# First stage of a transformer layer: conditioning rows in three small buffers, and their transfers moved from SyncE's queue to GpSimd's

## The chip, the cores and the metric

The kernel runs on one core of a Trainium2 chip. The metric is the device time of one execution in microseconds (us). Five engines work side by side, each through its own instructions in order: TensorE (PE in the profile, its weight loads PEld), VectorE (DVE), ScalarE (ACT), GpSimd (POOL) and SyncE (SP), which only issues transfers. Transfers (DMAs) from HBM to the core's memory SBUF run on 16 DMA engines that all queues share.

## The reference, cut to what matters

One layer over 256 tokens of width 2048, in float32. A condition vector `c` makes nine modulation vectors of 2048 numbers each (three triples of shift, scale and gate); a feed-forward block, a token mixer and a second feed-forward block follow, each with a layer norm behind it.

```python
def _swiglu(h, w_in, w_out):
    gate, up = jnp.split(h @ w_in, 2, axis=-1)
    return (jax.nn.silu(gate) * up) @ w_out

def _layer(x, c, w_ada, b_ada, ffn1_w_in, ffn1_w_out, ln1_g, ln1_b, w_in, ...):
    ada = (jax.nn.silu(c) @ w_ada + b_ada)[:, None, :]
    sh1, sc1, g1, sh2, sc2, g2, sh3, sc3, g3 = jnp.split(ada, N_ADA, axis=-1)
    h = _swiglu(_modulate(x, sh1, sc1), ffn1_w_in, ffn1_w_out)
    x = _layernorm(ALPHA * x + 0.5 * (1 + g1) * h, ln1_g, ln1_b)
    h = _token_mixer(_modulate(x, sh2, sc2), w_in, ...)
    x = _layernorm(ALPHA * x + (1 + g2) * h, ln2_g, ln2_b)
    h = _swiglu(_modulate(x, sh3, sc3), ffn2_w_in, ffn2_w_out)
    x = _layernorm(ALPHA * x + 0.5 * (1 + g3) * h, ln3_g, ln3_b)
    return x
```

`w_ada` is 2048 x 18432, `ffn1_w_in` and `ffn2_w_in` 2048 x 11264, the output weights 5632 x 2048. Nearly all bytes are weights, each read once.

## The kernel before, in words

**Weights.** Every weight comes in 1 MB transfers into one of three places of the tag "raw" (line 362). ScalarE rounds it to a high part `hi`, VectorE subtracts to get the low part `lo` (`split`, lines 141 to 143), each in six places, and TensorE makes three products of every pair (`mm3`, lines 372 to 375), so that float32 accuracy is kept. A "raw" place is free again when both of its `lo` parts are made.

**Ada rows.** A modulation vector pair or a half gate takes 16 rows (each 128 x 1024, 512 KB) of `w_ada`. VectorE multiplies each by one column of silu(c) and adds it up (`ada_acc`, lines 153 to 158); TensorE then sums over the partitions. In all there are 288 rows: 64 in the first stage, 224 behind it. Outside the first stage, `ada_pair` (lines 173 to 192) and `ada_gate` (lines 194 to 212) load rows into two places of the tag "araw". They are generators: `pump` (line 228) lets them make so many rows for every megabyte of weights that the other stages use, `need` (line 238) makes them finish a part. `pinned` orders what they issue on VectorE behind the latest weight split. A gate part also loads its bias over GpSimd's queue (line 203).

**First stage** (lines 656 to 786). The first feed-forward block starts before its modulation is whole. The 2048 inputs are cut into four quarters `j`. Quarter `j` needs 512 columns of shift and scale; `first_ada(j)` makes them from 16 rows and then modulates. The loop runs 12 calls of `first_in(j, i)` for each `j`; each uses 1 MB of weights (`first_w`, line 722) in 48 matmuls of 256 columns. Beside quarter `j` runs `first_ada(j + 1)`, one step after most calls (not after `i` = 4, 9, 11). A step loads two rows and adds up both. In steps 2 and 5 of 8 the two rows go to "araw", in the other six together into one "raw" place, the same three that the weights use (lines 663 to 675). Beside `j` = 3 the smaller mixer inputs are loaded and `pump` begins.

**Order.** All transfers but the six bias loads are issued by SyncE, in order: a transfer that waits for its place holds up all that come behind it. The order of the instructions on each engine is set when the program is built.

Of the kernel before, what the change touches and what calls it, by code (L numbers as in the profile page):

```python
# [7 lines left out]
F32 = mybir.dt.float32  # L8
# [7 lines left out]
P = 128  # L16
# [18 lines left out]
def layer_kernel(  # L35
# [8 lines left out]
    V, S, G_, PE, SP = nc.vector, nc.scalar, nc.gpsimd, nc.tensor, nc.sync  # L44
# [16 lines left out]
    ap = ctx.enter_context(tc.tile_pool(name="ap", bufs=1))  # L61
# [88 lines left out]
    def pair_cols(v, j):  # L150
        return w_ada[0, :, v * D:(v + 2) * D].rearrange("k (v n) -> k v n", v=2)[:, :, j * 512:(j + 1) * 512]

    def ada_acc(acc, raw, k):
        if k == 0:
            V.tensor_scalar_mul(acc, raw, csil[:, k:k + 1])
        else:
            V.scalar_tensor_tensor(out=acc, in0=raw, scalar=csil[:, k:k + 1], in1=acc,  # L157
                                   op0=ALU.mult, op1=ALU.add)


    def ada_split(acc, tag):
        ahi = ap.tile([P, 512], F32R, tag="ahi", name=f"ahi{tag}")
        alo = ap.tile([P, 512], F32R, tag="alo", name=f"alo{tag}")
        split(acc, ahi, alo)
        return ahi, alo

    def ada_sum(parts, tag):
        bc = aux_tile(f"bc{tag}")
        for i in range(2):
            PE.matmul(bc, onesr, parts[i], start=i == 0, stop=i == 1)  # L170
        return bc

    def ada_pair(v, js):
        for j in js:
            src = pair_cols(v, j)
            acc = ap.tile([P, 2, 512], F32, tag="acc", name=f"acc{v}_{j}")
            for k in range(KD):
                raw = ap.tile([P, 2, 512], F32, tag="araw", bufs=2, name=f"ar{v}_{j}_{k}")
                SP.dma_start(raw, src[k * P:(k + 1) * P])
                ada_acc(acc, raw, k)  # L180
                yield
            for i in range(2):
                parts = ada_split(acc[:, i, :], f"{v}_{j}_{i}")
                for _ in range(2):
                    yield PAUSE
                bc = ada_sum(parts, f"{v}_{j}_{i}")
                dg = ap.tile([P, 4, P], F32, tag="alo", name=f"dg{v}_{j}_{i}")
                V.tensor_tensor(out=dg, in0=bc.rearrange("p (a b) -> p a b", b=P),
                                in1=ident.unsqueeze(1).to_broadcast([P, 4, P]), op=ALU.mult)
                V.tensor_reduce(out=scsh[:, v + i, j * 4:(j + 1) * 4], in_=dg, axis=AX.X, op=ALU.add)  # L190
            cs = scsh[:, v:v + 2, j * 4:(j + 1) * 4]
            V.tensor_tensor(out=cs, in0=cs, in1=bcol[:, v:v + 2, j * 4:(j + 1) * 4], op=ALU.add)

    def ada_gate(v, s):
        for j in range(2):
            c0 = v * D + j * 1024
            acc = ap.tile([P, 1024], F32, tag="acc", name=f"acc{v}_{j}")
            for k in range(KD):
                raw = ap.tile([P, 1024], F32, tag="araw", bufs=2, name=f"ar{v}_{j}_{k}")
                SP.dma_start(raw, w_ada[0, k * P:(k + 1) * P, c0:c0 + 1024])  # L200
                ada_acc(acc, raw, k)
                yield
            G_.dma_start(gate[:, j * 1024:(j + 1) * 1024], b_ada[0:1, c0:c0 + 1024].to_broadcast([P, 1024]))
            for i in range(2):
                parts = ada_split(acc[:, i * 512:(i + 1) * 512], f"{v}_{j}_{i}")
                for _ in range(2):
                    yield PAUSE
                bc = ada_sum(parts, f"{v}_{j}_{i}")
                gs = gate[:, j * 1024 + i * 512:j * 1024 + (i + 1) * 512]
                V.scalar_tensor_tensor(out=gs, in0=bc, scalar=1.0, in1=gs, op0=ALU.add, op1=ALU.add)  # L210
                if s != 1.0:
                    V.tensor_scalar_mul(gs, gs, s)
# [176 lines left out]
    def ffn_in(w, xT, hT, j0, tag, npump):  # L389
        for j in range(j0, DFF // 256):  # L390
            ps = [mm_tile(f"gu_{tag}{j}_{f}") for f in range(2)]
            for gu in range(2):
                last = gu and j == DFF // 256 - 1
                cols_form_a(w, gu * DFF + j * 256, [p[:, gu * T:(gu + 1) * T] for p in ps], xT,
                            f"{tag}i{j}_{gu}", (lambda: None) if last else npump)
            for f in range(2):
                sg = sm.tile([P, T], F32, tag="sg", bufs=2, name=f"sg_{tag}{j}_{f}")
                S.activation(sg, ps[f][:, :T], AF.Silu)
                pin["h"] = V.tensor_tensor(out=hT[:, 2 * j + f, :], in0=sg, in1=ps[f][:, T:], op=ALU.mult).ins
        for _ in range(2):  # L400
            npump()
# [242 lines left out]
    def at(rate):  # L644
        return lambda: pump(rate)

    hp = tc.alloc_tile_pool(name="hp1", bufs=1)
    hT = hp.tile([P, KF, T], F32, name="hT1")
    h0 = [hp.tile([P, 2, T], F32R, name=f"h0_{i}") for i in range(2)]
    xp = tc.alloc_tile_pool(name="xp1", bufs=1, **right)  # L650
    npool = tc.alloc_tile_pool(name="np1", bufs=1, **right)
    xT = new_xT("f1")
    W1 = ffn1_w_in[0]


    def first_ada(j, ws=iter(())):
        src = pair_cols(0, j)
        if j % 2:
            acc = ap.tile([P, 2, 512], F32, tag="acc", name=f"acc0_{j}")
        else:  # L660
            acc = gate[:, :1024].rearrange("p (v n) -> p v n", v=2)
        for kk in range(8):
            if kk % 3 == 2:
                raws = []
                for h in range(2):
                    k = 2 * kk + h
                    raw = ap.tile([P, 2, 512], F32, tag="araw", bufs=2, name=f"ar0_{j}_{k}")
                    SP.dma_start(raw, src[k * P:(k + 1) * P])
                    raws.append(raw)
            else:  # L670
                raw = wp.tile([P, 2, 2, 512], F32, tag="raw", bufs=3, name=f"ar0_{j}_{kk}")
                for h in range(2):
                    k = 2 * kk + h
                    SP.dma_start(raw[:, h], src[k * P:(k + 1) * P])
                raws = [raw[:, h] for h in range(2)]
            for h in range(2):
                k = 2 * kk + h
                if k < KD - 1:
                    ada_acc(acc, raws[h], k)
                else:  # L680
                    for b in range(2):
                        bs = slice(b * 256, (b + 1) * 256)
                        ada_acc(acc[:, :, bs], raws[h][:, :, bs], k)
            if kk == 5:
                mb = modulate_both(0, j, rs0, xT)
            if kk in (5, 6):
                next(mb)
            yield
        cps = aux_tile(f"cp{j}"), mm_tile(f"cq{j}")

        def column(q):
            cp = cps[q % 2][:, q:q + 2]
            for v in range(2):
                PE.matmul(cp[:, v:v + 1], acc[:, v, q * P:(q + 1) * P], ones[:, 0:1], start=True, stop=True)
            k = 4 * j + q
            V.tensor_tensor(out=scsh[:, 0:2, k:k + 1], in0=cp.unsqueeze(2), in1=bcol[:, 0:2, k:k + 1], op=ALU.add)

        column(0)
        next(mb)
        column(1)  # L700
        next(mb)
        next(mb)
        column(2)
        next(ws, None)
        next(mb)
        column(3)
        next(mb)
        next(ws, None)
        for _ in mb:
            pass  # L710
        yield
# [10 lines left out]
    def first_w(j, i):  # L722
        c0 = (i % 2) * DFF + i // 2 * 512
        for k, hi, lo in load_w(W1[j * 512:(j + 1) * 512, c0:c0 + 512], 4, 512, f"s{j}_{i}"):
            yield 4 * j + k, hi, lo
# [52 lines left out]
    for j in range(4):  # L778
        fa = first_ada(j + 1) if j < 3 else load_mixer_smalls()
        for i in range(NS):  # L780
            first_in(j, i, ws if i + j == 0 else first_w(j, i))
            for _ in range(i not in (4, 9, 11)):
                with pinned():
                    next(fa, 0)
            if j == 3 and i > 2:
                pump(R_F)
    npool.release()
    ffn_in(W1, xT, hT, NS, "f1", at(R_IN))
    xp.release()
    lnp = tc.alloc_tile_pool(name="ln1", bufs=1, **right)  # L790
# [45 lines left out]
    fence, _, xs = boundary(*ent["f"], lgb, 3, "1", xT, entry_of(mo_load, mow, 3, 6), KD)  # L836
# [326 lines left out]
    for j in (2, 3, 0, 1):  # L1163
        ps = form_a_pair(C_FQ + j * 256, C_FK + j * 256, f"f{j}")
        for i in range(2):
            h = 2 * j + i
# [88 lines left out]
    for j in range(2, 10):  # L1255
# [8 lines left out]
        for f in range(2):  # L1264
            i = 2 * j + f
# [11 lines left out]
    for j in range(2, 10):  # L1277
# [7 lines left out]
        for f in range(2):  # L1285
            i = 2 * j + f
# [51 lines left out]
```

## Time and profile before

| | us |
|---|---|
| median of three runs | 1966.2 (1963.88 to 1972.04) |
| the profiled execution, its own time | 1965.57 |
| span of the profiled execution | 1963.8 |
| PE busy / DVE busy / ACT busy / POOL busy | 1896.5 / 1495.8 / 961.1 / 6.3 |
| first matmul of the first stage, last one | 37.8, 320.5 |

HBM was read at 259 GB/s over the span (506.71 MB). A profile is read here by engine and by stage: a share of busy time over the span says little where stages have different limits. In rows of windows, the count behind "x" is the number of instructions that touched the window; for PE it is the better measure, since the ends of matmuls are modelled.

### The profile page before, as it was taken

The page shows a single profiled execution, that of the slowest core. Times are in us where ns is not written, and L with a number is a line of the kernel's source. Part 1 is how long each engine was busy: PE and PEld are TensorE (multiplying, and loading weights), DVE is VectorE, ACT ScalarE, POOL GpSimd, SP SyncE. Part 2 cuts the span into 40 slices and gives each one's busy share as a digit, 9 for nine tenths or more (in the row PEclk, how much of TensorE's full clock was granted, in tenths as well). Part 3 has the DMA queues.
Part 4 walks back from the last instruction along what each step waited for, and adds up shares of the span by engine and source line. Part 5 has one row for each costly group of instructions (what it writes and reads, how often), then busy time and mean ns, then how long its engine had stood idle before and what let it go on. Part 6 is the DMA issues. An engine that isn't in the chain of part 4 may idle for free.

```text
span 1963.8 us, 32259 instructions
## 1 busy us (share of the span) xinstructions
PE 1896.5 (97%) x13057; PEld 1727.6 (88%) x13057; DVE 1495.8 (76%) x1878; ACT 961.1 (49%) x1396; POOL 6.3 (0%) x17
## 2 busy tenths in 40 slices
PE   3999999999999999899999998999999999999997
PEld 3999999999988888588999786899999999988885
DVE  7788889777788897678888688777766655555776
ACT  3644354443454554745755544555444444444553
POOL 0000000000000000000000000000000000000000
PEclk9999999999999999999999999999999999999999
DMA  9998978899898786489888784888777765655552
GB/s 331 342 315 278 314 253 289 290 305 326 281 343 303 268 303 208 140 292 319 270 300 278 273 285 151 285 292 274 241 248 249 261 216 190 236 193 193 193 193 86
DMA packets 301820, 510.89 MB, mean 260 GB/s; under 512 B 10818, under 2 KB 158690, under 8 KB 300648
## 3 DMA queue, kind: packets, MB, share of 16 engines
q1 hardware_dynamic: 300808, 505.70, 76.2%
q0 software_dynamic: 864, 3.15, 0.5%
q8 instruction: 102, 1.67, 0.4%
q14 instruction: 46, 0.38, 0.0%
HBM read 506.71 MB, written 2.10 MB: 259 GB/s over the span
## 4 chain that ended last, share of the span: by engine, by line
PE 83%; DVE 8%; DMA 5%; ACT 2%; issue 2%; SPq 0%; DVEq 0%; ACTq 0%
PE gu_f L374 8%; PE gu_f L375 8%; PE gu_f L373 8%; PE o_f L373 8%; PE o_f L375 8%; PE o_f L374 8%; PE s L373 3%; PE s L375 3%; PE s L374 3%; DMA raw_s<-in_ffn_w_in_dram 2%; DVE lo_s L143 2%; PE fs L375 1%; PE fs L374 1%; PE fs L373 1%; PE o_mx L373 1%
## 5 line engine op out<-in xcount | busy, mean ns | idle before, releaser
L157 DVE SCALAR_TENSOR_TENSOR acc<-ar,csil,acc 128x1024 f32<-128x1024 f32 x242 | 307.8, 1272 | 74.6 <-DMA ar<-in_w_ada_dram 72.9
L373 PE MATMUL s<-xhi_f,hi_s 128*128 128x256 f32 x768 | 215.0, 280 | 3.0 <-ACT hi_s L142 3.0
L375 PE MATMUL s<-xhi_f,lo_s 128*128 128x256 f32 x768 | 214.4, 280 | 1.9 <-DVE lo_s L143 1.9
L374 PE MATMUL s<-xlo_f,hi_s 128*128 128x256 f32 x768 | 214.2, 279 | 0.0
L375 PE MATMUL gu_f<-xhi_f,lo_f2i 128*128 128x256 f32 x768 | 212.0, 276 | 0.0
L373 PE MATMUL gu_f<-xhi_f,hi_f2i 128*128 128x256 f32 x768 | 212.0, 276 | 0.0
L374 PE MATMUL gu_f<-xlo_f,hi_f2i 128*128 128x256 f32 x768 | 212.0, 276 | 0.0
L143 DVE TENSOR_TENSOR lo_f2i<-raw_f2i,hi_f2i 128x1024 fp32r<-128x1024 f32 x96 | 117.6, 1225 | 91.4 <-ACT hi_f2i L142 91.4
L373 PE MATMUL gu_f<-xhi_f,hi_f1i 128*128 128x256 f32 x640 | 176.8, 276 | 0.0
L375 PE MATMUL gu_f<-xhi_f,lo_f1i 128*128 128x256 f32 x640 | 176.7, 276 | 0.0
L374 PE MATMUL gu_f<-xlo_f,hi_f1i 128*128 128x256 f32 x640 | 176.7, 276 | 0.0
L142 ACT CAST hi_f2i<-raw_f2i 128x1024 fp32r<-128x1024 f32 x96 | 100.8, 1050 | 135.4 <-PE gu_f L374 124.6
L373 PEld LDWEIGHTS s<-xhi_f,hi_s 128*128 128x128 f32 x768 | 146.2, 190 | 3.5 <-ACT hi_s L142 3.4
L142 ACT CAST hi_s<-raw_s 128x1024 fp32r<-128x1024 f32 x96 | 96.6, 1049 | 107.0 <-DMA raw_s<-in_ffn_w_in_dram 85.9
L375 PEld LDWEIGHTS s<-xhi_f,lo_s 128*128 128x128 f32 x768 | 145.9, 190 | 2.9 <-DVE lo_s L143 2.8
L374 PEld LDWEIGHTS s<-xlo_f,hi_s 128*128 128x128 f32 x768 | 146.4, 191 | 0.0
L374 PEld LDWEIGHTS gu_f<-xlo_f,hi_f2i 128*128 128x128 f32 x768 | 144.2, 188 | 0.2
L373 PEld LDWEIGHTS gu_f<-xhi_f,hi_f2i 128*128 128x128 f32 x768 | 144.2, 188 | 0.2
L375 PEld LDWEIGHTS gu_f<-xhi_f,lo_f2i 128*128 128x128 f32 x768 | 144.2, 188 | 0.0
L142 ACT CAST hh<-hT 128x512 fp32r<-128x512 f32 x130 | 80.0, 622 | 127.9 <-PE o_f L374 126.6
L143 DVE TENSOR_TENSOR lo_f2o<-raw_f2o,hi_f2o 128x1024 fp32r<-128x1024 f32 x88 | 107.7, 1224 | 44.9 <-ACT hi_f2o L142 44.8
L143 DVE TENSOR_TENSOR lo_s<-raw_s,hi_s 128x1024 fp32r<-128x1024 f32 x96 | 114.5, 1221 | 30.6 <-ACT hi_s L142 30.6
(452 smaller groups left out, 5385.2 us busy)
## 6 DMA issues: line engine op xcount, KB each, us to landing
ar<-in_w_ada_dram SPq DMA_DIRECT2D x288, 512.0 KB, 5.4
raw_s<-in_ffn_w_in_dram SPq DMA_DIRECT2D x48, 1024.0 KB, 6.1
raw_f2i<-in_ffn_w_in_dram SPq DMA_DIRECT2D x48, 1024.0 KB, 5.2
raw_f1o<-in_ffn_w_out_dram SPq DMA_DIRECT2D x44, 1024.0 KB, 7.4
raw_f2o<-in_ffn_w_out_dram SPq DMA_DIRECT2D x44, 1024.0 KB, 5.1
raw_f1i<-in_ffn_w_in_dram SPq DMA_DIRECT2D x40, 1024.0 KB, 7.7
raw_mxo<-in_w_out_dram SPq DMA_DIRECT2D x16, 1024.0 KB, 6.1
raw_fh<-in_ffn_w_in_dram SPq DMA_DIRECT2D x16, 1024.0 KB, 7.3
```

The source lines that it names most:

```text
L142: S.copy(hi, src)
L143: return V.tensor_tensor(out=lo, in0=src, in1=hi.bitcast(F32), op=ALU.subtract)
L157: V.scalar_tensor_tensor(out=acc, in0=raw, scalar=csil[:, k:k + 1], in1=acc, op0=ALU.mult, op1=ALU.add)
L373: PE.matmul(o, ah, bh, start=start, stop=False)
L374: PE.matmul(o, ah, bl, start=False, stop=False)
L375: PE.matmul(o, al, bh, start=False, stop=stop)
```

## The change

Three edits.

1. `first_ada` for `j` >= 1 no longer uses "raw". Its rows go to three places of 512 KB: two of "araw", and one of a new pool `ep1` (tag "aw") for every third row. The pool is released behind the first stage. `first_ada(0)` is as it was.
2. A step for `j` >= 1 is now one row, not two; the loop takes one or two steps after each call by a list of 12 numbers, 17 steps in all (16 rows and the tail) where it took 9 (8 pairs and the tail).
3. The transfers of ada rows are issued from GpSimd's queue: in `first_ada` for `j` >= 1, and in `ada_pair` and `ada_gate`, so 272 of the 288 rows.

```diff
@@ ada_pair
-                SP.dma_start(raw, src[k * P:(k + 1) * P])
+                G_.dma_start(raw, src[k * P:(k + 1) * P])
@@ ada_gate
-                SP.dma_start(raw, w_ada[0, k * P:(k + 1) * P, c0:c0 + 1024])
+                G_.dma_start(raw, w_ada[0, k * P:(k + 1) * P, c0:c0 + 1024])
@@ before the first stage
+    ep = tc.alloc_tile_pool(name="ep1", bufs=1)
@@ first_ada
         for kk in range(8):
-            if kk % 3 == 2:
+            if j or kk % 3 == 2:
                 raws = []
                 for h in range(2):
                     k = 2 * kk + h
-                    raw = ap.tile([P, 2, 512], F32, tag="araw", bufs=2, name=f"ar0_{j}_{k}")
-                    SP.dma_start(raw, src[k * P:(k + 1) * P])
+                    where, tag, n = (ep, "aw", 1) if j and k % 3 == 2 else (ap, "araw", 2)
+                    raw = where.tile([P, 2, 512], F32, tag=tag, bufs=n, name=f"ar0_{j}_{k}")
+                    (G_ if j else SP).dma_start(raw, src[k * P:(k + 1) * P])
                     raws.append(raw)
+                    if j and h == 0:
+                        ada_acc(acc, raw, k)
+                        yield
...
-            for h in range(2):
+            for h in range(j > 0, 2):
@@ the loop over j and i
-            for _ in range(i not in (4, 9, 11)):
+            for _ in range((2, 1, 2, 1, 2, 2, 1, 2, 1, 2, 1, 0)[i] if j < 3 else i not in (4, 9, 11)):
                 with pinned():
                     next(fa, 0)
...
     npool.release()
+    ep.release()
```

## The prediction

> **What bounds the kernel now.** I read the page's totals first, then windows of ten us through the first stage, then the waits there. On the page, TensorE is busy almost throughout.
>
> ```profile
> span 1963.8 us, 32259 instructions
> PE 1896.5 (97%) x13057; PEld 1727.6 (88%) x13057; DVE 1495.8 (76%) x1878; ACT 961.1 (49%) x1396; POOL 6.3 (0%) x17
> ```
>
> So 1963.8 - 1896.5 = 67 us of TensorE idleness is all that a change of transfers could win, most of it before the first matmul and in the norms. What the first stage holds of it shows in windows (columns: window and length, then busy time and count of PE, PEld, DVE, ACT, POOL, granted clock, DMA share, GB/s).
>
> ```profile
> 50.00:60.00 10.00, 10.00 (x90) 10.00 (x89) 8.00 (x7) 5.01 (x7) 0.00 (x0) 1.00 0.93 342
> 150.00:160.00 10.00, 9.45 (x84) 9.25 (x82) 8.38 (x10) 0.04 (x1) 0.00 (x0) 1.00 0.94 322
> 160.00:170.00 10.00, 7.93 (x52) 7.72 (x53) 8.66 (x9) 6.99 (x8) 0.00 (x0) 0.83 0.85 276
> 210.00:220.00 10.00, 9.67 (x85) 9.47 (x85) 9.96 (x11) 4.00 (x4) 0.00 (x0) 1.00 0.93 317
> 230.00:240.00 10.00, 8.72 (x74) 8.32 (x74) 7.76 (x10) 4.41 (x5) 0.00 (x0) 1.00 1.02 361
> 240.00:250.00 10.00, 8.96 (x79) 8.76 (x78) 8.88 (x11) 5.58 (x6) 0.00 (x0) 1.00 0.90 306
> 38.00:258.00 220.00, 214.50 (x1831) 212.91 (x1832) 183.87 (x205) 104.40 (x135) 0.67 (x1) 0.99 0.88 305
> ```
>
> The full rate is 90 matmuls in 10 us. The five poor windows lack 6, 38, 5, 16 and 11 of them, 76 in all, at 9.0 per us 8.4 us: the ceiling of what this stage can win. The clock fell to 0.83 in the worst one, so part of its price is the clock. Who was late:
>
> ```profile
> ACT hi_s L142 <- DMA raw_s<-in_ffn_w_in_dram: 85.9, 28, 10.2
> SPq L363 <- DVE lo_s L143: 67.0, 29, 5.1
> SPq L363 <- DVE acc L157: 16.7, 6, 4.5
> SPq L363 <- DVE gate L157: 12.2, 3, 6.1
> ```
>
> These are waits between 40 and 258 us (total, times, longest). ScalarE waits for weights, and SyncE's weight transfers (L363) wait 16.7 + 12.2 = 28.9 us for an ada row to be added up (L157), because the row sits in a weight's place or at the queue's head. SyncE's queue around the worst stall:
>
> ```profile
> 147.61 0.37 SPq L668 DMA_DIRECT2D ar<-in_w_ada_dram  x1
> 148.74 1.21 SPq L674 DMA_DIRECT2D ar<-in_w_ada_dram  x2
> ...
> 153.47 10.59 SPq L363 DMA_DIRECT2D raw_s<-in_ffn_w_in_dram  x4
> 167.15 0.88 SPq L674 DMA_DIRECT2D ar<-in_w_ada_dram  x2
> ...
> 160.22 1.99 ACT L142 CAST hi_s<-raw_s 128x1024 fp32r<-128x1024 f32 x2 [10.18 <-DMA raw_s<-in_ffn_w_in_dram]
> ```
>
> Two rows take a "raw" place at 148.74; the next weight goes out only at 153.47, and ScalarE, idle for 10.18 us, starts at 160.22. The rows cause the stall.
>
> **The change part by part.** *Places.* A quarter is 12 x 48 = 576 matmuls, 64 us at 9.0 per us. Before, 12 weights and 6 row pairs share three places: 64 / 18 x 3 = 10.7 us for each use. After, 12 weights: 16 us. The landings, in the order weights (whole stage), ada rows (40 to 258 us), ada rows (330 to 745 us), GpSimd's two bias loads (170 to 335 us), all six bias loads, min/median/max; last the row additions of 330 to 745 us (count | busy, mean ns | idle before):
>
> ```profile
> DMA to landing us min/median/max: 4.9/6.1/9.2
> ...
> DMA to landing us min/median/max: 3.9/5.8/9.0
> ...
> DMA to landing us min/median/max: 3.9/5.3/9.3
> ...
> DMA to landing us min/median/max: 4.3/6.7/9.0
> ...
> L203 POOL DMA_DIRECT2D gate<-in_b_ada_dram x6: 527/530/667, 178.6 to 1208.5; - x6
> ...
> DMA to landing us min/median/max: 4.1/5.0/9.0
> ...
> L157 DVE SCALAR_TENSOR_TENSOR acc<-ar,csil,acc 128x1024 f32<-128x1024 f32 x78 | 100.0, 1281 | 36.1 <-DMA ar<-in_w_ada_dram 35.9
> ```
>
> Two rows' landing of 5.8 and their two additions of 1.28 fill 8.4 of 10.7 us before any wait in VectorE's order, and half of 16, so the stalls by place go. But at 230 to 250 us the DMA share was 1.02 and 0.90: there the engines themselves were full, and those 16 + 11 matmuls, with the 5 at 210 (share 0.93), I leave. What I take away is 6 + 38 = 44 matmuls, 4.9 us; bounds 0 and 8.4.
>
> *Rows in three small places.* 16 rows through three places in 64 us leave 12 us for each use; the worst bias landing, 9.0, and one addition of 1.28 are 10.3. VectorE does the same additions. Cost 0, hidden in that 12 us; if landings pass 10.7 us VectorE waits at the row, and behind it the `lo` parts, then TensorE.
>
> *Issue.* 272 issues at GpSimd's 0.53 us are 144 us on an engine busy for 6.3 us: nothing waits for it, cost 0. What stands in that queue besides: the six bias loads and the mask's two instructions.
>
> ```profile
> 330.14 0.53 POOL L203 DMA_DIRECT2D gate<-in_b_ada_dram  x1 [150.92 <-DVE hT L748]
> 673.16 0.53 POOL L203 DMA_DIRECT2D gate<-in_b_ada_dram  x1 [342.49 <-DVE o_f L436]
> 834.53 0.81 POOL L855 MEMSET mask<- 128x256 f32 x1 [45.41 <-DVE xlo_mx L355]
> ...
> 1023.78 9.42 SPq L200 DMA_DIRECT2D ar<-in_w_ada_dram  x4
> ```
>
> The bias loads waited there for `gate` to be free. Behind their part's 16 rows they come later than that: the one of 673.16 moves behind the last row of its part, which SyncE issued about 1025, one of the four rows of that line. So no row queues behind a waiting bias, and the bias has two pauses of the pump until it is used; the mask, now behind rows pumped beside the projection ahead of it, is wanted only in attention. Cost 0, bounds 0 and +1.
>
> *Landing from the other queue.* A row's place is reissued when its addition is done, so outside the first stage, with two places, a later landing goes into VectorE's order. No row of `w_ada` went over GpSimd's queue, so the nearest rows bound it: all bias loads against rows of 330 to 745 us, 5.0 - 5.3 = -0.3 us by the medians, 9.0 - 5.3 = +3.7 at the worst. I take the pair under like load, 6.7 - 5.8 = +0.9 us. What covers it:
>
> ```profile
> 330.00:745.00 415.00, 415.00 (x2741) 377.50 (x2741) 342.74 (x362) 196.59 (x238) 1.06 (x2) 1.00 0.90 303
> ...
>   DMA ar<-in_w_ada_dram: 35.9, 30
> ...
> L142 ACT CAST hi_f1i<-raw_f1i 128x1024 fp32r<-128x1024 f32 x73 | 75.6, 1049 | 86.4 <-PE gu_f L374 59.9 <-DMA raw_f1i<-in_ffn_w_in_dram 23.8 <-DVE lo_f1i L143 1.3
> ```
>
> From 330 to 745 us TensorE never idles, and ScalarE waits 59.9 us for TensorE to free a `hi` place: the parts are made ahead. VectorE idles 415 - 342.7 = 72.3 us, of which 35.9 are 30 waits for rows; 36.4 us are spare. Thirty waits longer by 0.9 us are 27 us: hidden, but barely. For moments when several fall together I charge +2 us; bounds 0 and 30 x 3.7 - 36.4 = +75. In the mixer and behind it rows wait likewise, with their own spare; the one place where TensorE itself waits for a row is this:
>
> ```profile
> 1316.77 0.37 SPq L179 DMA_DIRECT2D ar<-in_w_ada_dram  x1
> ...
> 1322.90 1.28 DVE L157 SCALAR_TENSOR_TENSOR acc<-ar,csil,acc 128x1024 f32<-128x1024 f32 x1 [0.84 <-DMA ar<-in_w_ada_dram]
> ...
> 1324.22 0.62 ACT L142 CAST ahi<-acc 128x512 fp32r<-128x512 f32 x1 [1.69 <-DVE acc L157]
> ...
> PE bc L170 <- ACT ahi L142: 1.9, 1, 1.9
> ```
>
> The last row of the last shift and scale part is issued at 1316.77, landing 1322.90 - 1316.77 = 6.1 us later, and TensorE loses 1.9 us. With +0.9 it loses 2.8: +0.9, bounds -1.9 (landing 4.1) and +2.9 (landing 9.0).
>
> The Trainium skill has a rule against this whole edit: on its page "DMA: Bandwidth & Descriptors", section "Issuing engines are not separate DMA queues", transfers of all queues run on the same 16 engines, and a second issuer saves only the sequencer's time. By it the first stage would win nothing from the queue, only from the places; it has a rival below.
>
> *Sum.* Against the profiled 1965.57 (span 1963.8 and 1.8 around it, 0.6 below the median of 1966.2): -4.9 + 2 + 0.9 = -2.0, so 1963.6; beside the median 1964.
>
> **The rivals.**
>
> *A, the two-place stream slows VectorE (slower).* If a row lands later by more than 36.4 / 30 = 1.2 us, so after 6.5 us instead of 5.3, VectorE has no spare time between 330 and 745 us; the `lo` parts come late and TensorE starves. For it speaks the busy moment of a bias load:
>
> ```profile
> 332.00:333.00 1.00, 1.00 (x12) 1.00 (x11) 1.00 (x2) 1.00 (x2) 0.00 (x0) 1.00 0.96 306
> 333.50:334.50 1.00, 1.00 (x11) 1.00 (x11) 1.00 (x2) 0.07 (x1) 0.00 (x0) 1.00 1.03 242
> 334.50:335.50 1.00, 1.00 (x12) 1.00 (x11) 1.00 (x2) 0.00 (x0) 0.00 (x0) 1.00 0.81 236
> ```
>
> This load, issued at 330.14, is the one of 9.0 us, and while two queues had work the rate fell from 306 to 242 and 236 GB/s. Against it: rows over SyncE reach 9.3 too, and the median bias load takes 5.0. The Trainium skill, same page, section "Queues, rings and completion order", has each engine take turns between its queues packet by packet, so that a row shares with a weight in flight; the landing of 9.0 fits that, and no row here shows the turns. Halfway between +0.9 and +3.7, +2.3: 30 x 2.3 - 36.4 = +33, less 4.9: 1994.
>
> *B, all stalls go (faster).* The engines' full shares at 230 to 250 us were themselves a catching up after late issues; then 8.4 us go, and the landing of 4.1 us takes the 1.9 us at 1324: 1965.6 - 10.3 = 1955. Against it: the stage moves 305 GB/s now, and at the full rate 90 x 220 / 10 = 1980 matmuls instead of 1831, so 330; single windows reached 361.
>
> *C, mixing costs the first stage bandwidth (slower).* If two queues at once lose what those windows show, 67 GB/s in two of the load's 9 us, some 15 of 305, the 220 us grow by 5%, 11 us, and the 4.9 stay: 1977.
>
> *D, no effect on the stalls.* The queue only changes who issues, and the weights, sent earlier, land later by as much. No 4.9: 1968.5. It is what the Trainium skill's rule on issuing engines, named above, would make of the queue. Against it: 28.9 us of waits for rows do vanish from SyncE's queue.
>
> **How the numbers follow.** Forecast 0.40, A 0.32, B 0.14, C 0.08, D 0.06. The bound of 0.5%, about what a measurement of this kernel tells from no change, is 9.8 us: below 1956.4 is faster, above 1976 slower. B lies across its bound, 0.10 beyond it; A and C count as slower, with 0.02 of the forecast's upper end: 0.42. The rest, 0.48, is no change. The forecast's own range is 1958 to 1975. A spreads from 1976 to 2040, a third of it above 2000; B's lower half is below 1955. The range of 8 in 10 leaves out these two, 0.11 and 0.07: 1955 to 2000.
>
> **What would show it.** The sums for the last quarter's modulation end the stage's first three quarters (duration, then first and last start):
>
> ```profile
> L694 PE MATMUL cp<-trir,acc x16: 164/250/271, 102.1 to 250.5; 128*128 128x1 f32 x16
> ```
>
> Right: its last start some 5 us before 250.5; SyncE's weight waits on L157 in the first stage gone, windows 150 to 170 at 90 matmuls; row landings of 330 to 745 us at a median near 6.2; TensorE still without idle time there. For A: a median above 6.5 and windows there under their counts, with VectorE's waits for rows well over 72 us in all. For C: the first stage under 305 GB/s with DMA shares no lower. The forecast is wrong if any stage but the first and the place at 1324 moves by more than 3 us.

## The result, and the profile after

| | before | after |
|---|---|---|
| median, us (lowest to highest) | 1968.1 (1963.9 to 1972.0) | 2013.8 (2009.7 to 2019.6) |
| ratio to the kernel before (95% interval) | 1 | 1.0232 (1.0210 to 1.0253) |
| profiled execution: its time, span | 1965.6, 1963.8 | 2019.6, 2017.6 |

The change costs 2.3%, 45.7 us by the medians of four runs each. The profiled execution after is the slowest of its four, 5.8 us above their median, so the differences by stage below, 53.8 us in all, are those of this pair of executions. The forecast was 1964 with a range of 1955 to 2000, so it was wrong, and wrong in its range too.

Where the time went, from the first and the last matmul of each stage in the two traces (us; the mixer is reckoned from the end of the output projection before it to the end of its own):

```
                        before   after   difference
first stage              282.7   274.6     -8.1
rest of ffn1, inner      220.7   224.8     +4.1
ffn1 output              244.7   258.2    +13.5
mixer                    419.9   453.8    +33.9
first part of ffn2       152.0   160.7     +8.7
rest, to the end         592.9   592.9      0.0
```

The first matmul comes 1.4 us later after the change (39.2 us against 37.8), so the shorter first stage ends 6.7 us earlier. So the first stage did what it was changed for, and 60.2 us were lost in the four stages behind it, which the edit touches only through the queue of their ada rows. The totals of the profile after, and the chain of waits that ended last, by engine, of before and of after:

```profile
span 2017.6 us, 32352 instructions
PE 1909.5 (95%) x13057; PEld 1734.0 (86%) x13057; DVE 1494.3 (74%) x1878; ACT 958.9 (48%) x1396; POOL 184.5 (9%) x289
```
```profile
PE 83%; DVE 8%; DMA 5%; ACT 2%; issue 2%; SPq 0%; DVEq 0%; ACTq 0%
```
```profile
PE 53%; DMA 20%; issue 16%; DVE 9%; ACT 2%; POOL 0%; DVEq 0%; SPq 0%; POOLq 0%; ACTq 0%
DMA ar<-in_w_ada_dram 17%; PE gu_f L373 6%; PE gu_f L375 6%; PE gu_f L374 6%; PE o_f L373 5%; PE o_f L374 5%; PE o_f L375 5%; DVE acc L157 4%; PE s L373 4%; PE s L375 3%; PE s L374 3%; PE fs L374 1%; PE fs L373 1%; PE fs L375 1%; DVE lo_f1o L143 1%
```

VectorE and ScalarE did the same work. What is new is that the chain runs for 17% of the span through transfers of ada rows. The group of row additions, before and after (count | busy, mean ns | idle before and what ended it), and the line of the rows' transfers (issuer, count, size, median us to landing):

```profile
L157 DVE SCALAR_TENSOR_TENSOR acc<-ar,csil,acc 128x1024 f32<-128x1024 f32 x242 | 307.8, 1272 | 74.6 <-DMA ar<-in_w_ada_dram 72.9 <-DVE acc L157 0.3
...
ar<-in_w_ada_dram SPq DMA_DIRECT2D x288, 512.0 KB, 5.4
```
```profile
L157 DVE SCALAR_TENSOR_TENSOR acc<-ar,csil,acc 128x1024 f32<-128x1024 f32 x242 | 307.6, 1272 | 161.1 <-DMA ar<-in_w_ada_dram 159.7
...
ar<-in_w_ada_dram POOLq DMA_DIRECT2D x272, 512.0 KB, 5.5
```

VectorE waits 86.8 us more for rows (159.7 - 72.9), although a row lands 5.5 us after its issue where it landed 5.4 us after it. That pair of lines is the riddle of this case: the wait more than doubled with a landing that hardly moved.

Windows of the profile after that answer to those of the prediction (columns as there), then the longer ones of the later stages, first those of before:

```profile
150.00:160.00 10.00, 10.00 (x90) 10.00 (x90) 9.96 (x12) 3.63 (x4) 2.17 (x3) 1.00 0.93 331
160.00:170.00 10.00, 10.00 (x90) 10.00 (x89) 7.44 (x9) 3.52 (x4) 0.00 (x0) 1.00 0.90 312
210.00:220.00 10.00, 10.00 (x90) 10.00 (x90) 10.00 (x12) 4.11 (x4) 2.17 (x3) 1.00 0.96 349
230.00:240.00 10.00, 10.00 (x91) 10.00 (x90) 7.11 (x9) 2.93 (x3) 0.00 (x0) 1.00 0.84 281
240.00:250.00 10.00, 10.00 (x91) 10.00 (x90) 7.87 (x16) 6.57 (x12) 0.00 (x0) 1.00 0.59 204
330.00:745.00 415.00, 403.62 (x2639) 363.32 (x2638) 324.91 (x343) 185.60 (x227) 54.73 (x80) 1.00 0.86 292
...
797.00:1251.00 454.00, 419.26 (x2527) 359.38 (x2526) 339.64 (x535) 229.35 (x414) 54.52 (x84) 0.97 0.74 248
```
```profile
786.00:1206.00 420.00, 409.82 (x2528) 352.89 (x2526) 338.86 (x537) 229.71 (x414) 2.84 (x4) 0.99 0.80 268
```

All five poor windows of the first stage are at 90 matmuls and the full clock. From 330 to 745 us TensorE, which never idled before, now idles 415 - 403.6 = 11.4 us. In the mixer as many matmuls (2528 and 2527) take 34 us more, of which 34.7 - 10.2 = 24.5 us are idleness of TensorE ((454 - 419.3) against (420 - 409.8)), and the other 9.4 us are a longer busy time, at a granted clock of 0.97 where it was 0.99.

Who is late there? The waits of VectorE in the mixer, before and after, and then TensorE's waits after, from 540 to 1412 us (total, times, longest):

```profile
DVE acc L157 <- DMA ar<-in_w_ada_dram: 22.5, 23, 2.2
```
```profile
DVE acc L157 <- DMA ar<-in_w_ada_dram: 58.7, 45, 3.4
...
PE bc L170 <- ACT ahi L142: 6.5, 1, 6.5
PE o_f L374 <- DVE lo_f1o L143: 6.4, 7, 1.9
PE ptp L980 <- ACT s L975: 5.9, 3, 4.0
PE sps L1082 <- DVE dm L1088: 5.6, 1, 5.6
PE pr_m L375 <- DVE lo_m1b L143: 5.2, 1, 5.2
PE o_mx L373 <- DVE res L438: 4.4, 1, 4.4
```

VectorE's waits for rows grew by 36.2 us in the mixer, as the stage did by 33.9. Of the six waits of TensorE shown, only that of `bc` was there before, with 1.9 us. TensorE never waits for a row itself except at `bc`; it waits for weight splits (`lo_f1o`, `lo_m1b`), for attention's small results (`s`, `dm`) and for the residual of an output projection (`res`). An example of how a row gets into that: the addition that starts at 1027.96 us has waited 3.32 us for its row, and behind it in VectorE's order stand a weight split and, from 1030.30 us, the `dm` for which TensorE waits 5.6 us. The chain of waits of the profile after, in a burst of rows there (start, us, what):

```profile
929.02 1.29 DVE acc L157
930.31 0.29 issue
930.60 6.07 DMA ar<-in_w_ada_dram
936.67 0.03 issue
936.70 1.28 DVE acc L157
937.98 0.02 DVE scsh L192
938.00 0.31 issue
938.31 1.28 DVE acc L157
939.59 0.29 issue
939.88 5.42 DMA ar<-in_w_ada_dram
```

This is the round trip of a place: the addition ends at 930.31 and frees it, GpSimd issues the next row 0.29 us later, and the row lands after 6.07 us. VectorE meanwhile adds up the row of the other place, makes a split and some small results, and then stands still for the last 1.28 us. With two places and such a landing, a burst of rows cannot go faster than one row in half of (0.29 + 6.07 + 1.28), 3.8 us. Two questions were left: whether that longer round trip is what costs, and why VectorE runs into it more often.

### The profile page after: what moved, and what is told of

The parts are those of the page before. It is cut to its first block, busy times and chain, and to the rows that moved or that the text cites. A ratio compares the mean times of both kernels' runs of the same rounds, so it can differ in the third digit from the quotient of the medians.

```text
span 2017.6 us, 32352 instructions
## 1 busy us (share of the span) xinstructions
PE 1909.5 (95%) x13057; PEld 1734.0 (86%) x13057; DVE 1494.3 (74%) x1878; ACT 958.9 (48%) x1396; POOL 184.5 (9%) x289
## 4 chain that ended last, share of the span: by engine, by line
PE 53%; DMA 20%; issue 16%; DVE 9%; ACT 2%; POOL 0%; DVEq 0%; SPq 0%; POOLq 0%; ACTq 0%
DMA ar<-in_w_ada_dram 17%; PE gu_f L373 6%; PE gu_f L375 6%; PE gu_f L374 6%; PE o_f L373 5%; PE o_f L374 5%; PE o_f L375 5%; DVE acc L157 4%; PE s L373 4%; PE s L375 3%; PE s L374 3%; PE fs L374 1%; PE fs L373 1%; PE fs L375 1%; DVE lo_f1o L143 1%
## 5 line engine op out<-in xcount | busy, mean ns | idle before, releaser
L157 DVE SCALAR_TENSOR_TENSOR acc<-ar,csil,acc 128x1024 f32<-128x1024 f32 x242 | 307.6, 1272 | 161.1 <-DMA ar<-in_w_ada_dram 159.7
L142 ACT CAST hi_s<-raw_s 128x1024 fp32r<-128x1024 f32 x96 | 100.3, 1052 | 116.3 <-PE s L374 72.6
L179 POOL DMA_DIRECT2D ar<-in_w_ada_dram x128 | 92.5, 722 | 559.4 <-DVE acc L157 358.6
L374 PE MATMUL o_f<-lo_f1o,hh 128*128 128x512 f32 x344 | 135.1, 393 | 4.5 <-DVE lo_f1o L143 4.5
```

The source lines that it names most:

```text
L142: S.copy(hi, src)
L179: G_.dma_start(raw, src[k * P:(k + 1) * P])
L374: PE.matmul(o, ah, bl, start=False, stop=False)
```

## The experiments

A second difference between the traces does not show in any sum. VectorE's order of instructions is set when the program is built, and the queue of the later rows alone changes it: with rows on GpSimd's queue, the 192 additions of rows 65 to 256 stand 176 places further ahead between the weight splits, 0.9 of a split each on average (117 of them move ahead). How many weight splits stand ahead of rows 81 to 96, in VectorE's order:

```
before  118 118 120 121 122 123 124 125 127 127 129 129 131 132 134 134
after   118 118 119 119 121 122 123 124 125 126 127 128 129 130 134 134
```

An addition that stands earlier leaves less work between it and the addition that freed its place, so its wait is met sooner. That made theory T1, the order. T2 was the longer round trip, T3 that two queues disturb each other's transfers. Two runs exchange the orders: the first has the kernel before with the order of after, the second the reverse. The forcing (AT is the list of places):

```diff
+    no = mybir.DependencyInfo(mybir.DependencyClass.NoSync, mybir.DependencyReason.DATA)
+    for i, n in zip(AC[-224:-32], AT):
+        tc.add_manual_dep(i, LO[n - 1].name, no, reason="order")
+        tc.add_manual_dep(LO[n], i.name, no, reason="order")
```

The forcing holds these additions among the weight splits, and nothing else. The other 916 instructions of VectorE are placed anew by each build: counted in the traces, 147 of them stand among other splits in x1 than in e2, and 37 in x2 than in e1 (both explained below), although the additions stand alike. So the runs exchange the order of the additions, and not exactly that of all of VectorE.

**x1: the order exchanged, SyncE's queue.**

> The kernel before, every transfer on SyncE's queue, but VectorE's row additions 65 to 256 are forced into the places between the weight splits which they have in the changed kernel (in sum 176 splits earlier over 192 rows; nothing is added to the work). Theory T1 (the cost is the order of VectorE's instructions: additions planned closer together than two places can bring rows): slow like the changed kernel, about +50 us on the kernel before, since the changed kernel lost 60.0 us behind the first stage and this one keeps the old first stage: 2010 to 2030 us; additions wait for rows about 150 us in all. Theory T2 (the cost is the round trip through GpSimd's queue: 0.30 instead of 0.03 us from a place coming free to its issue, and 5.5 instead of 5.4 us to the landing): no change, 1964 to 1972 us. Theory T3 (two queues disturb each other's transfers): no change either, as there is one queue.

**x2: the order exchanged, GpSimd's queue.**

> The changed kernel, rows on GpSimd's queue, but VectorE's row additions 65 to 256 are forced back into the places between the weight splits which they have in the kernel before. T1: the whole loss behind the first stage (60.0 us) goes and the first stage's gain (8.1 us) stays, so 1956 to 1966 us, below the kernel before; additions wait for rows 75 to 95 us in all. T2 and T3: still 2005 to 2020 us, additions waiting about 150 us. A result near 1985 would say that order and round trip share the cost.

**e1: the first stage alone changed.**

> The changed kernel with its first stage as changed (three small places, those rows issued by GpSimd), and only the rows of the later stages back on SyncE's queue. All theories of the loss (T1, T2, T3) put it in the rows of the later stages, so all expect the first stage's gain alone: 8.1 us less in the first stage, stages behind it within 3 us of the kernel before, 1957 to 1963 us. If the loss came from the first stage's edits (rows or weights in another phase when it ends), it would stay: above 1990 us.

```diff
-                G_.dma_start(raw, ...)
+                SP.dma_start(raw, ...)
```

This is the changed kernel with that line in `ada_pair` and in `ada_gate`.

**e2: the later rows' queue alone changed.**

> The kernel before with one edit alone: the rows of the later stages are issued by GpSimd; the first stage is untouched. T1, T2 and T3: the loss of the later stages without the first stage's gain, 1968 + 55 to 65 = 2020 to 2033 us, slower than the changed kernel by about 8 us. If the loss needs the new first stage (its earlier end or its rows), near 1968 us.

Measured:

| run | median us | ratio to before (95%) | rows' queue later | additions' order |
|---|---|---|---|---|
| e1 | 1962.0 | 0.9969 (0.9955 to 0.9982) | SyncE | old |
| x1 | 1992.1 | 1.0119 (1.0091 to 1.0147) | SyncE | new |
| x2 | 1995.0 | 1.0134 (1.0107 to 1.0160) | GpSimd | old |
| after | 2013.8 | 1.0232 (1.0210 to 1.0253) | GpSimd | new |
| e2 | 2022.9 | 1.0271 (1.0241 to 1.0302) | GpSimd | new |

x1 and e2 have the old first stage, the others the new one. e1 gives back all that was lost: its stages behind the first are within 1 us of the kernel before. e2 loses without the first stage's help. So the loss comes from the later rows' queue. But x1 and x2 both came out halfway between what T1 and T2 had expected, so neither holds the loss alone. The order costs 1992.1 - 1968.3 = 24 us on SyncE's queue and 2013.8 - 1995.0 = 19 us on GpSimd's; the queue costs 1995.0 - 1962.0 = 33 us with the old order and 2022.9 - 1992.1 = 31 us with the new one. Together that is some 50 to 57 us; after against e1 shows 52, e2 against before 55. The two add up. The row additions in x1 and in x2 (line numbers are shifted by the forcing's lines):

```profile
L161 DVE SCALAR_TENSOR_TENSOR acc<-ar,csil,acc 128x1024 f32<-128x1024 f32 x242 | 307.6, 1271 | 115.4 <-DMA ar<-in_w_ada_dram 113.8 <-DVE acc L161 0.4 <-DVE gp L1034 0.3
```
```profile
L161 DVE SCALAR_TENSOR_TENSOR acc<-ar,csil,acc 128x1024 f32<-128x1024 f32 x242 | 307.7, 1272 | 136.1 <-DMA ar<-in_w_ada_dram 134.8 <-DVE ylo L145 0.2
```

In x1 rows go over the same queue as before, and VectorE waits 40.9 us more for them (113.8 - 72.9), with nothing changed but the order: that of the additions, and of the other instructions that the build moved with them.

**x0: the control.**

> The kernel before with its own places of the row additions forced, in the way that x1 and x2 force them: a control for that way alone. All theories: no change, 1964 to 1974 us. If forcing an order costs time by itself, above 1980 us, and the results of x1 and x2 shrink by as much.

Measured 1970.9 us, ratio 1.0002 (0.9986 to 1.0018): the forcing itself costs nothing that can be seen. In x0 only 1 of the other 916 instructions moved, so it does not test what the moved ones add in x1 and x2.

**x3 and x5: is it the length of the round trip?** To lengthen it on SyncE's queue alone, later rows were first cut into pieces, with the old order forced:

```diff
-                SP.dma_start(raw, src[k * P:(k + 1) * P])
+                for p in range(0, P, P // 2):
+                    SP.dma_start(raw[p:p + P // 2], src[k * P + p:k * P + p + P // 2])
```

> The kernel of e1 (changed first stage, later rows on SyncE's queue, 1962.0 us) with each later row's transfer cut into two of 64 partitions, issued one behind the other by SyncE, and VectorE's order held as it was. One queue, same bytes, same order: only the issue of the last piece comes later, by one SyncE issue of about 0.38 us. T2 (the length of a place's round trip is what costs): in x2 the round trip of the rows that VectorE waited for grew by about 0.6 us (5.9 to 6.5) and the time by 33 us, so 0.38 us makes about +21 us: 1975 to 1992 us. T3 (two queues disturb each other): 1960 to 1964 us. If a transfer in smaller pieces lands sooner than it is issued later, below 1970 us as well.

> As x3, with four pieces of 32 partitions: the last is issued about 1.15 us later. T2: 1.15 / 0.6 x 33 = +63 us if the slope holds, less where a row has slack: 2000 to 2030 us. T3: 1960 to 1964 us.

Measured 2171.4 us (ratio 1.1028, 1.0997 to 1.1058) and 2345.3 us (1.1910, 1.1879 to 1.1941). Neither theory had this, and the runs answer another question than theirs. The additions wait no longer for rows than before (71.4 us with two pieces, 58.1 with four); the weights do not come in time (x3; issuer, count, size, median us to landing):

```profile
raw_f1o<-in_ffn_w_out_dram SPq DMA_DIRECT2D x44, 1024.0 KB, 9.7
raw_f1i<-in_ffn_w_in_dram SPq DMA_DIRECT2D x40, 1024.0 KB, 9.9
```

They took 7.4 and 7.7 us in the kernel before. In x5 they take 6.8 and 8.1 us, so there a later landing is not the reason. What made the pieces so dear stays open, and it need not be the transfers alone: 397 of VectorE's other 916 instructions stand among other splits than in e1 in x3, and 452 in x5.

**x7 to x10: a longer hand-over.** A cleaner way is to hand the place back through another engine: GpSimd overwrites a part of the row's place after its addition, before SyncE may load it again. The queue, the transfers and the additions' order stay those of e1; the way from the addition to the issue grows. Of VectorE's other 916 instructions 8, 12, 20 and 58 stand elsewhere than in e1, in x7, x8, x9 and x10.

```diff
                 ada_acc(acc, raw, k)
+                G_.memset(raw[:, 0, :128], 0.0)
```

> The kernel of e1 (later rows on SyncE's queue, 1962.0 us), VectorE's order held as it was; but a later row's place is handed back through GpSimd, which overwrites 128 columns of it after the row's addition, before SyncE may load it again. Same transfers, one queue; only the round trip of a place grows, by a hand-over of about 0.3 us and the overwrite of about 0.4 us (a 128x256 fill takes 0.80 us), so 0.7 us, as long as x2's growth. T2 (the round trip's length is what costs, whatever makes it longer): as x2, 1985 to 2003 us, additions waiting 120 to 150 us for rows. T3 (the second queue disturbs transfers): 1960 to 1966 us.

> As x7 with 256 columns: an overwrite of 0.8 us, the round trip longer by about 1.1 us. T2: 1.1 / 0.7 x 33 = +52 us, 2000 to 2025 us, and more waits than in x7. T3: 1960 to 1966 us.

> As x7 with 512 columns overwritten. In x7 and x8 the overwrites took only 0.205 and 0.312 us and a place's hand-over 0.34 and 0.45 us, so their round trips grew by 0.31 and 0.42 us and cost about 4 and 5 us; here 0.52 us of overwrite and a hand-over of about 0.66 us are expected, a growth of 0.63 us, that of x2 (hand-over 0.30 instead of 0.03 us, issue 0.53 to 0.72 instead of 0.38 us). T2 (length of the round trip, with spare time that covers the first 0.4 us or so): 1985 to 2000 us, as x2. T3 (GpSimd's queue costs beyond the length of the round trip: its transfers meet the weights' otherwise): 1966 to 1976 us.

> As x9 with the whole row's place overwritten, 0.95 us and a hand-over of about 1.1 us, a growth of 1.07 us. T2: above x2, 2005 to 2035 us. T3: the slope of x7 and x8 (12 us per us) gives 1975 us, 1968 to 1985 us.

The first two came out smaller than meant, since the overwrite is quick. GpSimd's lines in x7, x8, x9 and x10 (count | busy, mean ns):

```profile
L185 POOL MEMSET ar<- 128x128 f32 x128 | 26.2, 205 | 585.9 <-DVE acc L161 411.6 <-DVE acc L159 109.5 <-issue 56.6
```
```profile
L185 POOL MEMSET ar<- 128x256 f32 x128 | 40.0, 312 | 578.7 <-DVE acc L161 406.1 <-DVE acc L159 109.4 <-issue 55.6
```
```profile
L185 POOL MEMSET ar<- 128x512 f32 x128 | 67.4, 527 | 549.5 <-DVE acc L161 381.9 <-DVE acc L159 83.7 <-issue 56.8
```
```profile
L185 POOL MEMSET ar<- 128x1024 f32 x128 | 122.4, 956 | 510.0 <-DVE acc L161 338.7 <-DVE acc L159 82.1 <-issue 56.8
```

The four medians stand in the next table. T2 failed as it was put on record: all four runs are faster than its ranges. T3's ranges held for x7 and x9; x8 lies 1.1 us above its range and x10 3.2 us. So the hand-over's length does not by itself account for x2's loss. What follows is a reading made after these results.

All six kernels of the next table have one order of the additions and the new first stage. The hand-over is the median from the end of the addition that frees a place to the next issue into it; the round trip goes on to the start of that row's addition, as a mean over the rows of 190 for which VectorE stood still by more than 0.15 us; all worked out from the trace of each run.

| run | queue | hand-over us | rows waited for | their round trip us | waits in all us | median us |
|---|---|---|---|---|---|---|
| e1 | SyncE | 0.03 | 59 | 5.73 | 68.9 | 1962.0 |
| x7 | SyncE | 0.34 | 69 | 5.98 | 79.8 | 1965.6 |
| x8 | SyncE | 0.45 | 71 | 5.87 | 81.7 | 1967.1 |
| x9 | SyncE | 0.66 | 85 | 6.10 | 100.3 | 1970.8 |
| x10 | SyncE | 1.09 | 98 | 6.34 | 118.9 | 1988.2 |
| x2 | GpSimd | 0.30 | 89 | 6.40 | 124.3 | 1995.0 |

Read by the hand-over, x2 stands out: x8 hands over later and costs 5 us against x2's 33. Read by the round trip, it falls in line: x10, with all later rows on SyncE's queue, has 0.61 us more than e1 and costs 26 us, x2 has 0.67 and costs 33. This round trip is taken over the rows that had to wait, so it describes the waits as much as it explains them. And the cost is no straight line: the first 31 us of added waits (x9) cost 8.8 us, the next 19 us (x10) 17.4. Some waits may be hidden by spare time, and then no longer; the 58 instructions that moved in x10 may also have a part in the jump.

The orders can be read in this way too: x1's round trip (5.76 us) is that of x0 (5.73 us), which has the same first stage and queue, but 72 rows are waited for instead of 58, 109.4 us in all instead of 69.9.

Why x2's round trip is longer than its hand-over says is argued, not shown: GpSimd needs 0.53 us (gate rows) to 0.72 us (pairs) for an issue that takes SyncE 0.33 and 0.37 us, and in x2 rows of 330 to 745 us land 5.5 us after their issue, where they take 5.4 in e1 and 5.0 in all four relay runs, x7 with its short hand-over as well as x10. No run sets that part alone. It leaves some 7 us of x2's 33 open (1995.0 - 1988.2; the ratios to before are 1.0134, 1.0107 to 1.0160, and 1.0087, 1.0056 to 1.0118, for x10). And the two do not lose in the same place: against e1, x10 loses 7.1 us in the output of ffn1 and x2 1.3, while in the mixer x2 loses 30.5 us to x10's 17.1 with nearly the same waits for rows there (49.2 and 50.6 us). Of these 13.4 us, 6.6 are busy time of TensorE, at a granted clock of 0.96 in x2 and 0.98 in x10. So a longer hand-over on one queue costs time too, but that the queue's 33 us are the round trip's alone is not shown.

T3 in its plain form, that two queues cost bandwidth, falls by the queues' own lines (q1 has SyncE's transfers, q0 GpSimd's). Before, then after (packets, MB, time as a share of 16 engines' span):

```profile
q1 hardware_dynamic: 300808, 505.70, 76.2%
q0 software_dynamic: 864, 3.15, 0.5%
```
```profile
q1 hardware_dynamic: 239112, 363.08, 53.3%
q0 software_dynamic: 40032, 145.77, 21.3%
```

Both make 508.85 MB in 0.767 x 1963.8 and 0.746 x 2017.6 us of all engines: 2.96 us for each MB, before and after.

**e3 and e6: what gave the gain.**

> First stage: the three small places and the new steps, but every row, there too, issued by SyncE. Nothing comes from GpSimd. Theory P (the places give the gain, as they leave the large ones to the weights): as e1, 1959 to 1964 us, the first stage 8 to 9 us shorter than before. Theory Q (the queue has a part in it: SyncE, waiting for a row's place, no longer holds back the weight transfers queued behind): 1964 to 1968 us, the first stage 2 to 6 us shorter.

> The kernel before with one edit: the first stage's rows from its 17th on are issued by GpSimd; they keep their places (two of three steps in the large ones shared with the weights), later rows stay on SyncE. Theory P: no gain, 1966 to 1971 us, stage 1 within 2 us of 282.7. Theory Q: 3 to 8 us less, 1960 to 1965 us.

e3 is e1 with `SP.dma_start(raw, ...)` in `first_ada` too; e6 is the kernel before with `(G_ if j else SP).dma_start` there and nothing else. Measured: e3 1958.8 us, ratio 0.9943 (0.9922 to 0.9964); e6 1978.5 us, 1.0048 (1.0030 to 1.0066). Theory Q falls: the three small places, with the steps of one row that came with them, give the whole gain, as the first stage takes 274.8 us in e3 and 274.6 in after. No run parts the places from the steps. Theory P had e3 right but for 0.2 us, and missed e6, where it expected no change: the queue without the places makes the first stage longer, 290.9 us. Why it is longer was not shown; the waits of SyncE's weight transfers for rows in the weights' places, which vanish in after, stay (e6, 40 to 265 us):

```profile
SPq L363 <- DVE acc L157: 19.2, 6, 5.8
SPq L363 <- DVE gate L157: 10.6, 3, 5.4
```

They were 16.7 and 12.2 us before. e3 is faster than both kernels; whether it is faster than e1 the intervals do not tell.

## Why the prediction was wrong

*First stage: right in kind, too small.* The term was -4.9 us with bounds of 0 and -8.4; measured -8.1. By its end the stage wins 6.7 us, as it starts later. What failed in it is the choice to leave the stalls of 210 to 250 us where they were, because the DMA engines were full there. They went: three windows at 90 matmuls and more, with shares of 0.96, 0.84 and 0.59. That fits rival B, which had the full engines as a catching up after weights that were held back. The last `cp` for the next quarter came at 243.8 us where some 245.5 was expected. And the gain is that of the places and steps (e3), not the queue's.

*Rows in three small places, cost 0: right*, by e3 and by the first stage of after.

*Issue by GpSimd, cost 0: wrong in what was counted.* The 272 issues were priced by whom they keep busy, and no one waits for GpSimd. But each lies inside a place's round trip: 0.53 to 0.72 us instead of 0.33 to 0.37, behind a hand-over of 0.30 us instead of 0.03. The 0.53 us were a bias load's; rows of a pair take 0.72.

*Bias loads and the mask in GpSimd's queue: no loss is seen.* No wait of the profile after names them.

*Landing from the other queue: the step that failed.* It read "Thirty waits longer by 0.9 us are 27 us: hidden, but barely", and charged 2. The price was not too low: the waiting rows' round trip grew by 0.67 us (e1 to x2), and the landing itself by 0.1. Three other things were. The thirty waits were those of one window; over all later stages 62 rows of 190 had been waited for by more than 0.15 us. The count was held fixed, though rows that just came in time now come late: 59 became 89, so that x2 adds 55 us of waits where 59 x 0.67 would be 40. And VectorE's order was held fixed, which the built program does not do: with the additions 0.9 of a split further ahead on average, and other instructions moved beside them, it cost another 41 us of waits and 24 us of time (x1). The mixer had one clause, "with their own spare", and lost 33.9 us; its row waits stand ahead of small products on which TensorE waits, so spare time of VectorE as a sum covers little there. Even from 330 to 745 us, TensorE idles by 11.4 us. The term's own upper bound, +75, had room for the loss; the charge and the range did not use it.

*The place at 1324 us.* TensorE's wait for `ahi` was to grow from 1.9 to 2.8 us, 4.8 at most; it is 6.5.

*The rivals.* A had the side right, and with 1994 us it came nearest. Its condition was not met: a landing above 6.5 us, where the median from 330 to 770 us is 5.6, and 5.5 over all rows; its sign, waits for rows well over 72 us, was. So the picture is A's, two places that cannot bring rows fast enough, entered by another door. B's picture of the first stage was right, its total not. C's lost bandwidth is not there. D fell with the stalls. But the rule named beside it, from the Trainium skill, "DMA: Bandwidth & Descriptors", section "Issuing engines are not separate DMA queues", agrees with this case in what it would make of the first stage, that nothing is won by the queue and only the places help: e3 has the gain without the second issuer, and each MB takes 2.96 us with either. The forecast named its own end: any later stage that moves by more than 3 us. Four did.

## What to carry to other kernels

A stream through two buffers is bound by the round trip of a place, so price a moved issue by what it adds between "place free" and "data there", not by whether the new issuer has time; then count again how many waits there are, since a longer trip makes new ones. An edit of a queue may also change the order in which other engines were planned, at a cost of its own: compare the instruction orders before comparing durations. Of a change with several edits, run each alone: here the buffers and their steps gave the gain (0.9943), and the issuer of the later rows cost 52 us beside it. And an order that is forced holds only for the instructions that it names: count in the trace what else moved.

## What had not been expected of the hardware

GpSimd's issue of a 512 KB row takes 0.72 us where the row is 2 x 512 columns of `w_ada` and 0.53 us where it is 1024 in one piece, SyncE's 0.37 and 0.33 us. Rows of 330 to 745 us on SyncE's queue land 5.4 us after their issue at a hand-over of 0.03 us (e1), and 5.0 us at 0.34 as at 1.09 us (x7, x10), so that a delay is not paid in full; why was not found. And the run that cut 512 KB transfers of 128 partitions into two of 64 took 209 us more than e1 (2171.4 - 1962.0), more than any wait in this study, though with much of VectorE's order changed beside it.
